# A decoder layer on one core: conditioning dots placed one per query block, and gate stores issued by ScalarE

## The chip, the cores and the metric

The kernel runs on one core of a Trainium2 chip. The core has five engines that run beside each other, each through its own list of instructions in order: TensorE (PE: matmuls, which write to PSUM, with the loads of its weights as PEld), VectorE (DVE), ScalarE (ACT), GpSimd (POOL) and SyncE (SP, which here only issues DMAs). Sixteen DMA engines move data between DRAM and the on-chip memory (SBUF). The metric is the device time of one execution in microseconds (us), as a median of several runs.

## The reference

One layer of a decoder: a token-mixing part (a convolution and a stick-breaking attention, merged by gates), then a SwiGLU part. Width and sequence length are 1024, with 8 heads of 64. What matters here is where the conditioning vector `c` goes in, and what the gates are:

```python
c_act = jax.nn.silu(c)
mod = c_act @ ada_w[l] + ada_b[l]
sh1, sc1, ga1, sh2, sc2, ga2 = [m[:, None, :] for m in jnp.split(mod, 6, axis=-1)]
h = rmsnorm(x, pre_mix_g[l]) * (1.0 + sc1) + sh1
y = hybrid_mixer(h, ...)
x = x + ga1 * rmsnorm(y, post_mix_g[l])
h = rmsnorm(x, pre_ffn_g[l]) * (1.0 + sc2) + sh2
y = swiglu_ffn(h, w_ffn_in[l], w_ffn_out[l])
x = x + ga2 * rmsnorm(y, post_ffn_g[l])
```

In `hybrid_mixer`, `merged = sigmoid(g_conv) * y_conv + sigmoid(g_att) * y_att`. Both sigmoids come from `h @ w_in`, as do the convolution's input and the queries, keys and values. In the attention, each key's weight is its own sigmoid times the product of (1 - sigmoid) over the keys between it and the query. So the scores of one block of queries pass through two sigmoids, a running product and a multiplication before they meet the values.

`sh1` and `sc1` are needed at once. `ga1`, `sh2` and `sc2` are not needed before the output projection of the mixer has been computed, and `ga2` only at the very end.

## The kernel before

The kernel keeps activations transposed: 8 tiles of 128 channels by 1024 tokens. Each operand of a matmul is split into a high and a low part (`hi`, `lo`), and a product is three matmuls. ACT mostly makes the high part (a copy with rounding), DVE or POOL the low one (a subtraction).

**Order of the work.** A scheduler builds each engine's list. It goes through the program with a modelled timeline, and gives an engine that is free the ready instruction that comes first in the program. `tc.high_priority(offset=...)` lets instructions count as if they came earlier; `SOONER` is 5000, and the attention (`head`) runs under it, so that it goes ahead of the products traced around it, which fill the gaps. On the chip each list then runs strictly in order, and so does SP's list of DMAs: a DMA that waits for its buffer or its data holds back all DMAs behind it.

**Stages.** (1) `sh1`, `sc1` and the normalised input, together with the first products (to line 291). (2) Attention with fillers (lines 318 to 564): for each of four pairs of heads `p`, the gated input of the convolution `glu(p)`, the transposed operands `t_ops`, the convolution `conv(p)`, and two heads by `attend`, with the next pair's queries and keys (`qk_pair`) in between. Behind the fourth pair come the last convolution, four plain gates (`PLAIN`), and the first two of seven products of six gate pairs (`GPAIRS`, lines 552 to 564). (3) The other five products of these gate pairs (`other_five`), with the layer norm of the convolution (`ln_all`) in between. (4) The convolution's projection `y_conv` for n = 0 to 7 (lines 697 to 722), then the attention's projection (lines 733 to 747). (5) The output projection and the SwiGLU part (from line 749 on).

**One head** (line 422) goes through four blocks `c` of 256 queries. For each half-block of 128 queries and up to 512 keys: PE computes scores `z`; ACT makes two sigmoids, `kap` and `beta` (lines 455 and 456); DVE turns `kap` into running products by a scan (line 459); POOL multiplies `beta` by them (line 461). Then PE transposes `beta` (line 471), ACT and DVE split the result into `ahi` and `alo` (lines 474 and 475), and PE multiplies both with the values (lines 480 and 481).

**The conditioning dots.** 32 columns of `mod` (16 to 47: `ga1`, `sh2`, `sc2`, `ga2`, eight each) are computed by `dot_c` (line 133): a weight tile of 128 x 1024 is loaded, and DVE multiplies it with the broadcast `cb` and sums along the row (line 135). Before, `ada2_dots(n)` (line 502) loads and computes `n` of them; it is called with 0, 4, 8 and 8 ahead of the four pairs of heads (line 536), with 2 behind each plain gate (line 546), and for what is left (line 547). The tiles have a tag of their own, `aw`, with two buffers. Nothing ties the dots to a place in DVE's list but their place in the program and those buffers. Lines 548 to 551 add the bias to all 32 columns and fold them with the norms' weights.

**The gate results.** Sigmoids of gates are written to DRAM (`s_d`, and a partial product in `e_d0`) and read back later. All these stores go through `load` (line 103), which issues on SP. Their source tiles (tag `sg`, two buffers, shared with the convolution's outputs) come free when the store has landed.

**Shared buffers.** The tag `wraw` has three buffers. Through them go the raw weights of all products by `load_w`, among them `wc` (convolution's projection) and `wa` (attention's projection), the gate pairs' weights (line 604) and the four `of` tiles with the attention's output (line 725).

Of the kernel before, what the change touches and what calls it, by code (L numbers as in the profile page):

```python
# [18 lines left out]
P = 128  # L19
# [31 lines left out]
SOONER = 5000  # L51
A2_AT = (0, 4, 8, 8)
EARLY = 9
# [22 lines left out]
def tile_block(ctx: ExitStack, tc: tile.TileContext, xT, vecs, crow, ada1, ada2, win, wv, wcv, wat, wo, w1, w2, cvw, out):  # L76
# [241 lines left out]
    with ExitStack() as sC:  # L318
        pc = mkpool(sC, "pc")
        with ExitStack() as sA:  # L320
# [101 lines left out]
            def head(p, hh, qst, kst, klo, vts, oT):  # L422
# [6 lines left out]
                for ci, c in enumerate(order):  # L429
# [5 lines left out]
                    for sc in range(nsc - 1, -1, -1):  # L435
                        probs = []
                        for i in (2 * c, 2 * c + 1):
# [20 lines left out]
                            init = 1.0 if diag else kap[:, s_hi:s_hi + 1]  # L458
                            dve.tensor_tensor_scan(rev, rev, rev, init, op0=ALU.mult, op1=ALU.bypass)  # L459
                            m = w - 1 if diag else w  # L460
# [21 lines left out]
                    if ci % 2 == 1:  # L482
                        cs = slice((c // 2) * CH, (c // 2 + 1) * CH)
                        act.activation(oT[half, cs], av[other], AF.Copy)
                        dve.tensor_tensor(oT[half, cs], av[half], oT[half, cs], op=ALU.add)  # L485

            def attend(p, qk, vts):
                qs, ks, kl = qk
                oT = pa.tile([P, T], F32, tag="oT", name=f"oT{p}", bufs=1)
                nxt = None  # L490
                for hh in range(2):
                    with tc.high_priority(offset=SOONER):
                        head(p, hh, qs[hh], ks[hh], kl[hh], vts, oT)
                    if hh == 0 and p < 3:
                        nxt = qk_pair(p + 1)
                with tc.high_priority(offset=SOONER):
                    load(o_d[p], oT)
                return nxt

            a2 = deque(range(2 * KT, 6 * KT))  # L500

            def ada2_dots(n):
                for _ in range(n):
                    col = a2.popleft()
                    w = pa.tile([P, D], F32, tag="aw", name=f"ada2_{col}", bufs=2)
                    load(w, ada2[col - 2 * KT])
                    dot_c(w, cb, col)
# [21 lines left out]
            for p in range(4):  # L529
                glu(p)  # L530
                if p == 2:
                    v = v_half(1)
                t_ops(p)
                if p < 3:
                    conv(p)
                ada2_dots(A2_AT[p])
                qk = attend(p, qk, v)
            conv(3)
            for n in PLAIN:
                gb = banks2(f"pg{n}")  # L540
                gemm(gb, load_w(win[20 + n], f"wg{n}"), h, range(KT))
                for c in range(NCH):
                    sg = sgp.tile([P, CH], F32, tag="sg", name=f"sg{n}_{c}", bufs=2)
                    act.activation(sg, gb[c], AF.Sigmoid, bias=0.0, scale=1.0)
                    load(s_d[n][:, c * CH:(c + 1) * CH], sg)
                ada2_dots(2)
            ada2_dots(len(a2))
            add_bias(16, 48)
            fold_gate(gpost1, 16, C_POST1)
            fold_scale(scale2, 32, C_PRE2)  # L550
            fold_gate(gpost2, 40, C_POST2)
            for i in GPAIRS:
# [5 lines left out]
                act.activation(e[0], k1, AF.Copy)  # L558
                load(e_d0[i], e[0])
                k2 = bank(f"k2_{i}")  # L560
                prod0(k2, w_op(f"a12_{i}", raw[:, CH:], act, pool), "B21")
                dve.tensor_tensor(e[1], k2, e[0], op=ALU.add)
                act.activation(e[1], e[1], AF.Sigmoid, bias=0.0, scale=1.0)
                load(s_d[2 * i][:, :CH], e[1])

    sV.close()
    with ExitStack() as sG:
# [45 lines left out]
        def sig_out(t, n, c):  # L613
            act.activation(t, t, AF.Sigmoid, bias=0.0, scale=1.0)
            load(s_d[n][:, c * CH:(c + 1) * CH], t)

# [104 lines left out]
        for n in range(KT):  # L721
            y_conv(n)
        ohi, olo = [], []
        for p in range(4):
# [573 lines left out]
```

## Time and profile before

| | |
|---|---|
| three runs | 1488.84, 1490.8, 1490.9 us; median 1490.8 us |
| the profiled execution | 1492.5 us |
| its span in the profile | 1490.7 us, 19082 instructions |
| DMA | 271.06 MB, mean 182 GB/s |

The prediction quotes rows of several views. A row of a *timeline* has the start, the busy time, engine, line, operation, output <- inputs, and in brackets the idle time of the engine before it with what ended it. A row by *stretch* has start:end and length, then the busy time of PE, PEld, DVE, ACT and POOL with the number of instructions, the clock granted to TensorE as a share of full speed, the share of time in which the 16 DMA engines were busy, and GB/s. A *wait* row says who waited for whom, for how long in total, how often, and the longest. Durations of an instruction are given as min/median/max in ns. "SPq" is SP's queue of DMA issues; "landing" is the time from a DMA's issue until its data have arrived.

### The profile page before, as it was taken

What the parts mean: (1) busy time and instruction counts of PE and PEld (TensorE: products, weight loads), DVE (VectorE), ACT (ScalarE), POOL (GpSimd) and SP (SyncE); (2) the same over time, 40 slices, a digit from 0 to 9 for tenths busy, and PEclk for the clock granted to TensorE, in tenths of its full rate; (3) what the DMA queues carried; (4) which work ended last, traced back from release to release, by engine and by line L of the source; (5) the groups of instructions that cost most, each with busy time, mean ns of one, the idle gap of its engine ahead of it and who ended that gap; (6) DMA issues with size and microseconds to landing.
All of it is one profiled execution on the core that took longest, in us unless ns stands there. A gap on an engine that the chain in (4) does not pass through costs nothing.

```text
span 1490.7 us, 19082 instructions
## 1 busy us (share of the span) xinstructions
PE 1402.0 (94%) x6888; PEld 1170.8 (79%) x6888; DVE 1016.2 (68%) x1440; ACT 654.3 (44%) x1138; POOL 310.5 (21%) x281
## 2 busy tenths in 40 slices
PE   5997999999999999899998949999999999999996
PEld 4886788898888777688886738887888887888886
DVE  7899877666481168837467697678778864764457
ACT  5363466446462335422445463334444443432541
POOL 0042535325162364333000000001111110000000
PEclk9999999999999999999999979999999999999999
DMA  9456444054045763643443623547777748666843
GB/s 383 167 186 189 151 155 144 26 184 134 23 142 195 278 210 122 232 157 109 152 145 132 224 92 128 170 156 264 258 249 259 255 134 287 235 227 193 286 128 113
DMA packets 98717, 271.06 MB, mean 182 GB/s; under 512 B 10048, under 2 KB 20416, under 8 KB 97600
## 3 DMA queue, kind: packets, MB, share of 16 engines
q1 hardware_dynamic: 88768, 235.24, 46.6%
q0 software_dynamic: 9856, 34.61, 6.0%
q8 instruction: 54, 0.88, 0.2%
q14 instruction: 39, 0.32, 0.1%
HBM read 196.41 MB, written 73.40 MB: 181 GB/s over the span
## 4 chain that ended last, share of the span: by engine, by line
PE 51%; DVE 4%; DMA 1%; ACT 0%; issue 0%; DVEq 0%; ACTq 0%
PE ka L892 14%; PE ka L1018 8%; PE kc L892 8%; PE pwo L180 5%; PE pb L1018 4%; PE pya L180 3%; PE pyc L180 3%; PE kb L892 2%; PE pa L1018 2%; PE ke L850 1%; DMA e_d<-e 1%; DVE y L831 1%; DVE e L855 0%; DMA w1u<-in_w_dram 0%; PE fsum L1225 0%
## 5 line engine op out<-in xcount | busy, mean ns | idle before, releaser
L461 POOL TENSOR_TENSOR be<-be,ka 128x127 f32<-128x127 f32 (+2 forms) x96 | 108.6, 1142 | 179.2 <-DVE ka L459 111.0
L459 DVE TENSOR_TENSOR_SCAN ka<-ka 128x128 f32<-128x128 f32 (+2 forms) x96 | 107.4, 1136 | 26.8 <-ACT ka L455 26.7
L107 POOL DMA_DIRECT2D g_d<-w x22 | 12.1, 552 | 413.1 <-DVE w L971 413.1
L455 ACT ACTIVATE ka<-z 128x128 f32<-128x128 f32 (+2 forms) x96 | 47.3, 495 | 66.5 <-PE z L454 30.8
L475 DVE TENSOR_TENSOR alo<-tr,ahi 128x512 fp32r<-128x512 f32 x80 | 52.8, 680 | 30.7 <-ACT ahi L474 30.5
L474 ACT ACTIVATE ahi<-tr 128x512 fp32r<-128x512 f32 x80 | 46.7, 602 | 39.7 <-PE tr L471 28.0
L892 PE MATMUL kc<-b,s4o 128*128 128x512 f32 x264 | 63.4, 389 | 0.0
L1018 PE MATMUL ka<-gt,w2f 128*128 128x512 f32 x264 | 63.4, 389 | 0.0
L1018 PEld LDWEIGHTS ka<-gt,w2f 128*128 128x128 f32 x264 | 49.6, 188 | 10.3
L892 PEld LDWEIGHTS kc<-b,s4o 128*128 128x128 f32 x264 | 49.6, 188 | 10.3
L471 PE MATMUL tr<-ident,be 128*128 128x128 f32 x288 | 50.6, 279 | 5.4 <-DVE alo L475 5.0
L850 PE MATMUL ke<-b,we_hi 128*128 128x512 f32 x144 | 50.0, 427 | 4.2 <-DVE b L161 2.5
L481 PE MATMUL av<-alo,vst 128*128 128x256 f32 x160 | 44.1, 299 | 9.3 <-DVE alo L475 9.2
L456 ACT ACTIVATE be<-z 128x128 f32<-128x128 f32 (+2 forms) x96 | 46.8, 498 | 10.1 <-PE tr L471 10.0
L135 DVE SCALAR_TENSOR_TENSOR ada<-ada,cb 128x1024 f32<-128x1024 f32 x32 | 45.2, 1414 | 8.2 <-DMA ada<-in_ada_dram 7.8
L180 PE MATMUL pwo<-mlo,wo_hi 128*128 128x512 f32 x128 | 50.2, 392 | 0.0
L180 PE MATMUL pwo<-mhi,wo_lo 128*128 128x512 f32 x128 | 50.2, 392 | 0.0
L180 PE MATMUL pwo<-mhi,wo_hi 128*128 128x512 f32 x128 | 49.8, 389 | 0.0
L480 PE MATMUL av<-ahi,vst 128*128 128x256 f32 x160 | 45.6, 299 | 1.7 <-DVE oT L485 1.2
L892 PE MATMUL ka<-b,a 128*128 128x512 f32 x156 | 40.7, 392 | 1.8 <-DVE a L883 1.8
L361 PE MATMUL pcv<-ph,cvw 128*128 128x128 f32 x320 | 41.6, 276 | 0.5 <-DMA ph<-v_d 0.5
L471 PEld LDWEIGHTS tr<-ident,be 128*128 128x128 f32 x288 | 35.5, 143 | 8.3 <-DVE alo L475 3.1
(484 smaller groups left out, 4127.6 us busy)
## 6 DMA issues: line engine op xcount, KB each, us to landing
w_d<-w2o POOLq DMA_DIRECT2D x44, 512.0 KB, 3.5
w2f<-w_d SPq DMA_DIRECT2D x44, 512.0 KB, 4.2
ada<-in_ada_dram SPq DMA_DIRECT2D x32, 512.0 KB, 3.7
w1g<-in_w_dram SPq DMA_DIRECT2D x22, 512.0 KB, 3.8
w1u<-in_w_dram SPq DMA_DIRECT2D x22, 512.0 KB, 4.3
w2r<-in_w_dram SPq DMA_DIRECT2D x44, 256.0 KB, 5.6
cvw<-in_cvw_dram SPq DMA_DIRECT2D x20, 512.0 KB, 3.8
ada_w<-in_ada_dram SPq DMA_DIRECT2D x8, 1024.0 KB, 12.3
```

What stands on the lines that cost most here:

```text
L180: pe.matmul(bank, st[:, cols], mv[k][:, c * CH:(c + 1) * CH], start=(i == 0 and s == 0), stop=(i == n - 1 and s == 2))
L455: act.activation(kap[:, s_lo:s_hi], z[:, zo:zo + w], AF.Sigmoid, bias=0.0, scale=-0.125)
L456: act.activation(beta[:, :w], z[:, zo:zo + w], AF.Sigmoid, bias=0.0, scale=0.125)
L459: dve.tensor_tensor_scan(rev, rev, rev, init, op0=ALU.mult, op1=ALU.bypass)
L461: pool.tensor_tensor(beta[:, :m], beta[:, :m], kap[:, s_lo + 1:s_lo + 1 + m], op=ALU.mult)
L471: pe.transpose(tr[:, o:o + P], src, ident)
L474: act.activation(ahi, tr, AF.Copy)
L475: dve.tensor_tensor(alo, tr, ahi, op=ALU.subtract)
L480: pe.matmul(avc, lhs, ahi[:, cols], start=(jp == c and jj == 0), stop=False)
L850: pe.matmul(kb, wf[st][:, cols], t[:, mv], start=(j == 0 and q == 0), stop=(j == HK - 1 and q == 2))
L892: pe.matmul(bank_, st[:, cols], t[:, mv], start=(first and j == 0 and s == 0), stop=(j == HK - 1 and s == 2), skip_group_check=not first)
L1018: pe.matmul(dst, w[st][:, cols], g[mv], start=first and s == 0, stop=last and s == 2, skip_group_check=more)
```

## The change

Three things are edited.

1. `head` becomes a generator. After each of its four blocks it hands back the block's last scan. In `attend`, from head 3 on (`2 * p + hh >= A2_HEAD` with `A2_HEAD = 2`, counted from 0), one dot follows each block: its load is traced with normal priority, and the dot itself stands in `tc.issue_after(scan.ins)`, which orders it behind that scan in DVE's list, without a wait between engines. That is 6 heads x 4 blocks = 24 dots, columns 16 to 39.
2. The last 8 dots (columns 40 to 47, `ga2`) follow the eight steps of `y_conv`, with their tiles in the tag `wraw`. The bias and the fold of these columns come after them; those of columns 16 to 39 stay where they were.
3. The 38 stores of gate results (8 of plain gates, 12 in the first two products of six gate pairs, 18 in `sig_out`) are issued by `act.dma_start`, on ACT's own DMA queue, instead of SP's.

```diff
-A2_AT = (0, 4, 8, 8)
+A2_HEAD = 2
...
-                            dve.tensor_tensor_scan(rev, rev, rev, init, op0=ALU.mult, op1=ALU.bypass)
+                            scan = dve.tensor_tensor_scan(rev, rev, rev, init, op0=ALU.mult, op1=ALU.bypass)
...
+                    yield scan
...
                 for hh in range(2):
+                    steps = head(p, hh, qs[hh], ks[hh], kl[hh], vts, oT)
+                    for _ in range(4):
+                        with tc.high_priority(offset=SOONER):
+                            scan = next(steps)
+                        if 2 * p + hh >= A2_HEAD:
+                            ada2_dot(scan)
                     with tc.high_priority(offset=SOONER):
-                        head(p, hh, qs[hh], ks[hh], kl[hh], vts, oT)
+                        assert next(steps, None) is None
...
-            a2 = deque(range(2 * KT, 6 * KT))
-
-            def ada2_dots(n):
-                for _ in range(n):
-                    col = a2.popleft()
-                    w = pa.tile([P, D], F32, tag="aw", name=f"ada2_{col}", bufs=2)
-                    load(w, ada2[col - 2 * KT])
+            a2 = deque(range(2 * KT, 5 * KT))
+
+            def ada2_dot(scan):
+                col = a2.popleft()
+                w = pa.tile([P, D], F32, tag="aw", name=f"ada2_{col}", bufs=2)
+                load(w, ada2[col - 2 * KT])
+                with tc.issue_after(scan.ins):
                     dot_c(w, cb, col)
...
-                ada2_dots(A2_AT[p])
...
-                    load(s_d[n][:, c * CH:(c + 1) * CH], sg)
-                ada2_dots(2)
-            ada2_dots(len(a2))
-            add_bias(16, 48)
+                    act.dma_start(s_d[n][:, c * CH:(c + 1) * CH], sg)
+            assert not a2
+            add_bias(16, 40)
             fold_gate(gpost1, 16, C_POST1)
             fold_scale(scale2, 32, C_PRE2)
-            fold_gate(gpost2, 40, C_POST2)
...
-                load(e_d0[i], e[0])
+                act.dma_start(e_d0[i], e[0])
...
-                load(s_d[2 * i][:, :CH], e[1])
+                act.dma_start(s_d[2 * i][:, :CH], e[1])
...
         def sig_out(t, n, c):
             act.activation(t, t, AF.Sigmoid, bias=0.0, scale=1.0)
-            load(s_d[n][:, c * CH:(c + 1) * CH], t)
+            act.dma_start(s_d[n][:, c * CH:(c + 1) * CH], t)
...
         for n in range(KT):
             y_conv(n)
+            w = wp.tile([P, D], F32, tag="wraw", name=f"ada2_{5 * KT + n}")
+            load(w, ada2[3 * KT + n])
+            dot_c(w, cb, 5 * KT + n)
+        add_bias(40, 48)
+        fold_gate(gpost2, 40, C_POST2)
```

## The prediction

> **What bounds the kernel now.** I read the page first, then the stretches, then the waits inside the stretches that the change touches.
>
> ```profile
> PE 1402.0 (94%) x6888; PEld 1170.8 (79%) x6888; DVE 1016.2 (68%) x1440; ACT 654.3 (44%) x1138; POOL 310.5 (21%) x281
> PE 51%; DVE 4%; DMA 1%; ACT 0%; issue 0%; DVEq 0%; ACTq 0%
> ```
>
> TensorE (PE) is busy for 1402.0 of 1490.7 us, and the chain that ended last runs mostly through it. None of its matmuls changes. The time can therefore only move where PE stands idle or runs at a reduced clock, and I look for these places. Here is the view of engine time by stretch (from and to, length, then busy time of PE, weight load, DVE, ACT and POOL, then the granted PE clock, DMA share, GB/s). The second fence is the same view for line 135 alone, the conditioning dots, and the third holds its durations:
>
> ```profile
> 60.00:176.00 116.00, 100.31 (x630) 87.35 (x630) 104.72 (x143) 53.17 (x108) 43.78 (x29) 0.96 0.60 191
> 176.00:456.00 280.00, 275.62 (x1696) 240.11 (x1695) 186.43 (x227) 157.44 (x322) 113.73 (x89) 1.00 0.34 113
> 540.00:628.00 88.00, 81.50 (x344) 64.19 (x344) 80.14 (x93) 46.15 (x68) 44.27 (x26) 0.99 0.46 157
> ```
>
> ```profile
> 60.00:176.00 116.00, 43.57 (x62) 0.96 0.60 191
> ```
>
> ```profile
> L135 DVE SCALAR_TENSOR_TENSOR ada<-ada,cb x32: 1191/1226/2108, 58.1 to 160.7; 128x1024 f32<-128x1024 f32 x32
> ```
>
> Stretch 60 to 176 holds the first V projection and heads 1 and 2. There VectorE (DVE) is busy for 104.72 of 116 us, and 43.57 us of that is dots (62 instructions, so 31 dots with their 31 accumulator reads: 1.41 us each). PE is idle for 116 - 100.31 = 15.7 us, and its clock averages 0.96, which costs another 0.04 x 116 = 4.6 us. In heads 3 to 8 (176 to 456) there is no dot, DVE is busy for 186.43 of 280 us (67%), and PE idles for 4.4 us at full clock. The waits of PE in the first stretch (who waited, for whom, total, times, longest) name the cause:
>
> ```profile
> PE av L481 <- DVE alo L475: 6.7, 6, 1.7
> PE tr L471 <- DVE alo L475: 4.8, 3, 2.7
> PE pv L381 <- DVE qst L405: 1.5, 2, 0.8
> PE z L451 <- ACT sg L290: 1.4, 1, 1.4
> ```
>
> 13.0 us of the 15.7 are waits for ordinary DVE work (`alo`, `qst`) that stands behind dots in a full, in-order queue. That is the first place. The second is at 491 us:
>
> ```profile
> 477.51 1.07 ACT L544 ACTIVATE sg<-pg 128x512 f32<-128x512 f32 x2
> ```
>
> ```profile
> 484.24 1.60 SPq L104 DMA_DIRECT2D s_d<-sg  x2
> ```
>
> ```profile
> DMA to landing us min/median/max: 8.9/9.2/9.5
> ```
>
> ```profile
> 488.11 0.39 PE L315 MATMUL k<-hhi,a 128*128 128x512 f32 x1
> ...
> 494.51 0.79 PE L315 MATMUL k<-hhi,a 128*128 128x512 f32 x1 [3.53 <-ACT sg L544]
> ```
>
> ```profile
> 495.00:500.00 5.00, 5.00 (x13) 3.84 (x13) 0.00 (x0) 0.08 (x1) 0.00 (x0) 0.50 0.99 395
> 500.00:505.00 5.00, 5.00 (x22) 4.05 (x22) 0.69 (x1) 2.39 (x4) 2.38 (x2) 0.93 0.39 75
> ```
>
> Two gate sigmoids end at 478.6. Their stores leave SP's queue only at 484.24, behind prefetches, and land 8.9 to 9.5 us later, at 493.7. Until then the two `sg` buffers are taken, so the next sigmoids cannot empty their PSUM banks, and PE waits 3.5 us. Then it runs at half clock: (1 - 0.50) x 5 + (1 - 0.93) x 5 = 2.9 us. Together 6.4 us.
>
> **The change part by part.**
>
> *A, 32 dots leave 60 to 176.* DVE there drops from 104.7 to about 61 us of 116 (53%). The loss was 15.7 + 4.6 = 20.3 us, or 0.65 us for each of the 31 dots. I keep 4.0: the 1.4 us wait for ScalarE (ACT), half of the `qst` wait (0.8), since those first evacuations come in a burst, and 1.8 for the rate of the later heads (4.4 / 280 x 116). Gain 16.3 us; bounds 8 (half) and 18.9 (all but the ACT wait). The 32 loads (32 x 512 KB) leave the stretch too, but at a DMA share of 0.60 nothing there waits for bandwidth. The bias and fold instructions that follow the last dot move out of this stretch as well.
>
> *B, 24 dots enter heads 3 to 8,* each behind the last scan of its query block. That adds 24 x 1.41 = 33.8 us: DVE goes from 186.4 to 220.2 of 280 us, 79%. Queued behind a dot stand the block's `alo` subtractions and the next block's scans, and PE, ACT and POOL wait for those. The next view shows what a loaded DVE costs PE, in stretches of 25 us:
>
> ```profile
> 75.00:100.00 25.00, 22.87 (x180) 21.59 (x180) 24.74 (x38) 16.27 (x35) 10.63 (x8) 1.00 0.60 187
> 100.00:125.00 25.00, 22.13 (x140) 19.06 (x138) 23.01 (x32) 9.55 (x21) 7.93 (x7) 1.00 0.54 171
> 200.00:225.00 25.00, 24.88 (x143) 20.84 (x142) 21.18 (x27) 16.06 (x34) 10.68 (x9) 1.00 0.50 182
> 225.00:250.00 25.00, 23.05 (x179) 20.90 (x178) 18.66 (x24) 17.02 (x40) 12.89 (x13) 1.00 0.45 138
> 275.00:300.00 25.00, 25.00 (x126) 20.30 (x125) 19.13 (x22) 12.43 (x26) 11.78 (x9) 1.00 0.00 1
> 400.00:425.00 25.00, 23.08 (x158) 20.06 (x157) 19.48 (x25) 15.66 (x35) 12.88 (x12) 1.00 0.19 64
> 425.00:450.00 25.00, 24.61 (x172) 22.11 (x171) 19.27 (x19) 16.48 (x38) 17.21 (x12) 1.00 0.56 169
> ```
>
> With DVE at 75 to 85% (the last five rows) PE idles 0.1, 2.0, 0, 1.9 and 0.4 us, 4.4 in all. About two dots, 3 us, come into each, which puts them at 87 to 97%, like the first two rows, where PE idles 2.1 and 2.9. At 2.5 each that is 12.5, so 8.1 us more than now. The six other stretches stay below 85% and add about nothing. A dot may float to a gap and is not bound to a crowded moment, so I take +7; bounds 0 and 24 x 0.65 = 15.6. The 24 loads are spread over 280 us, where the DMA share is 0.34. SP's queue holds each until the dot two before it has freed its buffer, and weight loads stand behind; blocks are 280 / 24 = 12 us apart, so I cost this at nothing. Without that cover it is part of the upper bound.
>
> *C, 38 stores move to ACT's queue* (8 plain gates, 12 in the six `B11`/`B21` pairs, 18 in `sig_out`). Issued right after their sigmoids, the stores of 478.6 land by 488.1 even if they still take 9.5 us, and the last plain gate's matmuls run into 488.1. The stall goes: -6 of 6.4. In exchange each issue holds ACT:
>
> ```profile
> L104 SPq DMA_DIRECT2D s_d<-gc x6: 319/327/424, 544.9 to 625.1; - x6
> ```
>
> ```profile
> SPq L104 <- ACT gc L614: 24.3, 5, 6.6
> ...
> SPq L104 <- ACT sg L544: 19.1, 5, 10.5
> ```
>
> No ACT issue exists in this trace; the row of SP gives 0.32 us, and I estimate 0.4 with the wait for ACT's own result: 38 x 0.4 = 15 us over some 175 us in which ACT is about half busy (46.15 of 88 in 540 to 628). What queues behind each issue are the next operand copies, for which PE's products wait. On the other side SP's loads no longer stand behind results of ACT (24.3 and 19.1 us of SP waiting in the two largest rows). I set these two against each other at 0, with -2 and +5 as bounds.
>
> *D, 8 dots and 8 loads of 512 KB enter the convolution's projection.*
>
> ```profile
> 618.00:668.00 50.00, 46.39 (x198) 38.01 (x197) 21.24 (x26) 12.51 (x14) 18.13 (x8) 0.97 0.67 240
> ```
>
> ```profile
> 603.53 4.52 SPq L104 DMA_DIRECT2D wc_raw<-in_wcv_dram  x2
> ```
>
> ```profile
> 616.11 2.40 POOL L169 TENSOR_TENSOR wc_lo<-wc_raw,wc_hi 128x1024 fp32r<-128x1024 f32 x1 [6.14 <-ACT wc_hi L159]
> ```
>
> ```profile
> 626.94 1.21 PE L180 MATMUL pyc<-clo,wc_hi 128*128 128x512 f32 x2 [3.61 <-DVE clo L654]
> ```
>
> ```profile
> 667.81 43.52 PE pya L180 x192
> ```
>
> ```profile
> ada<-in_ada_dram SPq DMA_DIRECT2D x32, 512.0 KB, 3.7
> ...
> yc<-s_d SPq DMA_DIRECT2D x8, 512.0 KB, 7.0
> ```
>
> From 628 on DVE has room (21.24 of 50 us busy). Two costs remain. First, PE enters this projection 3.6 us late behind DVE's `clo`, and before 628 DVE is full (80.14 of 88). Two of the three `wraw` buffers come free near 603 to 608, where two `wc` loads start now; two of the new loads can take them, and if their dots are ordered ahead of `clo` they cost up to 2 x 1.41 = 2.8. I take 1.5. Second, the eight tiles share those three buffers with the weights of both projections and the four `of` tiles, about 14 tiles before the first matmul of the attention projection (667.81). At 3.7 (landing of an `ada` load) + 1.4 each that is 14 / 3 x 5.1 = 24 us from 618.5, where the first weight's split ends and frees its buffer, and hidden; at 7.0 (a `yc` load) + 2.4 (POOL's part of a split) it is 44 us, to 662, which with the last split ends on the edge. I take 1.5, so +3 for D; bounds 0 and 18.
>
> Sum: -16.3 + 7 - 6 + 0 + 3 = -12.3 us. The profiled execution took 1492.5 us (span 1490.7), so it would become 1480.2. The median of the three runs is 1490.8, 1.7 below the profiled one, so 1490.8 - 12.3 = 1478.5. 0.2% of it, 3 us, is about what a measurement of this kernel can tell from no change.
>
> **The rivals.**
>
> *Heads 3 to 8 pay back the full price.* POOL's multiply after each scan has these rows in 60 to 176 and in 175 to 456:
>
> ```profile
> L461 POOL TENSOR_TENSOR be<-be,ka 128x512 f32<-128x512 f32 x8 | 15.3, 1927 | 14.3 <-DVE ka L459 11.2 <-ACT ahi L474 1.9 <-ACT be L456 1.2
> ```
>
> ```profile
> L461 POOL TENSOR_TENSOR be<-be,ka 128x512 f32<-128x512 f32 x24 | 31.0, 1304 | 44.0 <-DVE fo L524 18.6 <-DVE ka L459 11.2 <-ACT be L456 10.6
> ```
>
> Beside dots it takes 1.93 us, without them 1.30. The change puts each dot exactly where the multiply of the last scan starts: 24 x 0.62 = 15 us on the attention's chain, and the same 15.6 comes from 0.65 per dot. The result is -12.3 + 8.6 = -3.7, so 1487. For it: the two rows. Against it: in 176 to 456 PE has matmuls of other products between, and most delays of the chain cost it nothing. The Trainium skill, page "SBUF — State Buffer", section "Who interferes with whom", says that a DVE instruction with two SBUF inputs and a GpSimd instruction that reads SBUF exclude each other for the whole instruction, the later one waiting. By that rule a dot that starts first delays the multiply by its whole length; the two rows agree in sign with half of it.
>
> *The early idle time goes only by half,* since what moves up into the freed DVE (the transposed operands' subtractions) or ACT's own evacuations then end last: -12.3 + 8.1 = -4.2, so 1486.6. Against it: DVE falls to 53%, and ACT is busy for only 53.17 of 116.
>
> *Slower: the ring of three `wraw` buffers in the projections.* If the two early tiles keep their buffers until DVE has finished `clo` at 628, and loads land in 9.2 us as in the crowded time at 484, each of 14 tiles holds a buffer for about 9.2 + 2.4 = 11.6 us: 14 / 3 x 11.6 = 54 us from 628, so 682, plus 2.4 for the split of the first attention weight: 684.4 instead of 667.81, 16.6 us of idle PE. In place of the 1.5 counted for the ring that gives -12.3 + 15.1 = +2.8, and with one spell at half clock after it (2.9, as at 495) +5.7, so 1496.5. It decides the sign once the attention projection begins over 13.8 us later against the entry into the first projection. Against it: the DMA share in 618 to 668 is 0.67 on the mean, so loads should land faster than at 484.
>
> **How the numbers follow.** The forecast has 0.55, the full price in heads 3 to 8 0.2, the half gain 0.13, the ring 0.12. The second and third lie at 1487 with a spread of some 4 us, so a third of them falls within 3 us of no change; of the ring's cases a sixth does. Faster: 0.55 + 0.14 + 0.09 = 0.78; same: 0.06 + 0.04 + 0.02 = 0.12; slower: 0.10. Low end: A at 18.9, B at 0, C at 6.4, D at 0 would be 25.3 less, 1465.5; I stop at 1467. High end: the second and third rival with their spread, 1491, which leaves out most of the ring. The forecast's own part is 1468 to 1487.
>
> **What would show it.** Line 135 has nothing between 60 and 176 except what the queueing allows after head 2, 24 executions in heads 3 to 8, and 8 near the convolution's projection. In the first stretch PE's waits for `alo` fall from 11.5 to a few us, the clock reads 1.00, and heads 3 to 8 begin some 16 us earlier. PE idles 8 to 14 us in heads 3 to 8, with `alo` as releaser. The wait for `sg` of 3.5 us is gone, with no row of 0.50 behind it. PE enters the convolution's projection after at most 6 us of waiting. The forecast is wrong if PE still waits for `alo` in heads 1 and 2, if heads 3 to 8 idle above 15 us, or if the attention projection opens with a wait for `of` or `wa`.

## The result, and the profile after

The changed kernel takes 1496.98 us (median of 4 runs, 1495.33 to 1498.88), the kernel before 1489.82 on the same chip: ratio 1.0049, 95% interval 1.0037 to 1.0062. It is 7.2 us slower; the forecast was 12.3 us faster. The profiled execution took 1495.33 us, span 1493.6.

By stretch (columns as before), the changed kernel:

```profile
60.00:176.00 116.00, 108.16 (x690) 95.32 (x689) 70.92 (x88) 59.76 (x118) 36.42 (x30) 0.99 0.19 60
176.00:456.00 280.00, 269.34 (x1645) 232.35 (x1644) 219.17 (x266) 150.11 (x310) 127.84 (x88) 0.99 0.47 155
...
495.00:500.00 5.00, 0.51 (x1) 0.50 (x2) 0.00 (x0) 1.66 (x4) 3.71 (x3) 0.53 1.03 410
500.00:505.00 5.00, 5.00 (x13) 3.85 (x12) 0.69 (x1) 0.63 (x1) 0.00 (x0) 0.50 1.01 404
505.00:510.00 5.00, 5.00 (x22) 4.08 (x22) 0.69 (x1) 1.86 (x3) 1.29 (x1) 0.95 0.51 178
```

Read it as the prediction did, as *loss*: idle PE time plus (1 - clock) x length. In 60 to 176 it falls from 20.3 to 7.8 + 1.2 = 9.0 us, although DVE is now busy for only 71 of 116 us. In 176 to 456 it rises from 4.4 to 10.7 + 2.8 = 13.5. Of the 11.3 gained, 9.1 are gone again. (The clock is given to two digits, so a loss is good to 0.6 us in the first stretch and to 1.4 us in the second.) The stall near 490, which should have disappeared, has grown. PE's waits:

```profile
PE tr L471 <- DVE alo L475: 7.1, 5, 3.0
PE av L481 <- DVE alo L475: 4.6, 2, 3.0
PE pk L180 <- ACT wk_hi L159: 1.6, 1, 1.6
...
PE k L315 <- ACT ee L562: 7.3, 1, 7.3
PE lnm L675 <- POOL la L673: 4.0, 1, 4.0
PE k L315 <- DVE s4o L302: 3.8, 1, 3.8
```

The 3.5 us of waiting for `sg` have become 7.3 us for `ee`, a spell at half clock again behind it. ACT's own row of instructions tells why (timeline; ACTq is its queue of DMA issues):

```profile
484.17 1.07 ACT L550 ACTIVATE sg<-pg 128x512 f32<-128x512 f32 x2
485.13 0.63 ACT L159 ACTIVATE a<-ew 128x512 fp32r<-128x512 f32 x1
492.67 1.60 ACTq L551 DMA_DIRECT2D s_d<-sg  x2
494.40 1.67 ACT L159 ACTIVATE a<-ew 128x512 fp32r<-128x512 f32 x3 [8.64 <-DMA T4o<-t_d]
498.84 0.60 ACT L562 ACTIVATE ee<-k 128x512 f32<-128x512 f32 x1 [2.77 <-DMA s_d<-sg]
```

The sigmoids of the last plain gate run at 484.17, but their stores are issued only at 492.67. In between ACT does nothing for 8.64 us: 6.9 us until the first store is issued, the rest with the two issues. The profile puts the wait down to a load that has nothing to do with the stores: `T4o`, issued by SP. The trace's records of semaphores (counters on which a wait can stand) show the tie. In each kernel of this study, all DMAs that SP and ACT issue (540 here) count their landing on the same eight semaphores, and none is issued before the last one on its semaphore has landed. The store of 492.67 shares its semaphore with the `T4o` load issued at 480.87, which landed at 492.59; the second store, of 493.95, with one that landed at 493.87. Behind the waiting stores stand the operand copies (`a<-ew`) and the evacuation `ee`, for which PE waits. The `T4o` loads take

```profile
DMA to landing us min/median/max: 10.2/10.7/11.7
```

A second view is the path. From the timelines I take the starts of the first `z` product, of the first product on `T2o` (521.99 before, 522.01 after) and of the first `pya` (667.65 and 672.23), and the end of the span:

| kernel | z to T2o | T2o to pya | pya to end | loss 60-176 | loss 176-456 |
|---|---|---|---|---|---|
| before | 440.7 | 145.7 | 823.0 | 20.3 | 4.4 |
| changed | 441.2 | 150.2 | 821.3 | 9.0 | 13.5 |
| dots only | 445.4 | 146.4 | 820.1 | 13.0 | 13.3 |
| stores only | 440.3 | 149.1 | 824.9 | 19.5 | 4.4 |
| projection's 8 dots only | 433.0 | 145.8 | 819.5 | 14.3 | 4.3 |
| dots only, whole heads | 432.5 | 147.6 | 820.3 | 3.4 | 11.2 |

In the two profiled executions the difference is 2.9 us of span; the one before was 2.7 us above its median and the one after 1.6 below, which makes up the rest of the 7.2. So the first path, which should have shrunk by 15.3 us (A, B and C), is unchanged, and the second has grown by 4.5. (The split between the two depends a little on where the lists put the first `T2o` product; their sum does not.)

Each row is one execution, and the times of the kernel before in the second group of experiments alone lie between 1486.7 and 1494.0 us. In heads 1 and 2 the changed kernel and dots only have the same lists (551 of 553 matmuls from 81 to 176 stand in the same order) and nearly the same idle time, 7.8 and 8.4 us; their losses, 9.0 and 13.0, differ by the clock. A few us in one row carry little weight.

### The profile page after: what moved, and what is told of

Read it like the earlier page. It is cut to its first block, busy times and chain, and to the rows that moved or that the text cites. A ratio compares the mean times of both kernels' runs of the same rounds, so it can differ in the third digit from the quotient of the medians.

```text
span 1493.6 us, 19061 instructions
## 1 busy us (share of the span) xinstructions
PE 1399.3 (94%) x6888; PEld 1167.1 (78%) x6888; DVE 1025.0 (69%) x1441; ACT 656.0 (44%) x1138; POOL 316.1 (21%) x281
## 4 chain that ended last, share of the span: by engine, by line
PE 48%; DVE 5%; DMA 3%; issue 1%; ACT 1%; DVEq 0%; SPq 0%; ACTq 0%
PE ka L901 12%; PE ka L1027 8%; PE kc L901 7%; PE pwo L180 5%; PE pb L1027 4%; PE pya L180 3%; PE pyc L180 3%; PE ke L859 2%; PE pa L1027 2%; PE kb L901 2%; DMA w2r<-in_w_dram 1%; DMA w1u<-in_w_dram 1%; DMA e_d<-e 1%; ACT y L841 0%; PE k L315 0%
## 5 line engine op out<-in xcount | busy, mean ns | idle before, releaser
L461 POOL TENSOR_TENSOR be<-be,ka 128x127 f32<-128x127 f32 (+2 forms) x96 | 115.9, 1217 | 169.8 <-DVE ka L459 83.1
L459 DVE TENSOR_TENSOR_SCAN ka<-ka 128x128 f32<-128x128 f32 (+2 forms) x96 | 115.4, 1220 | 33.0 <-ACT ka L455 32.8
L901 PEld LDWEIGHTS kc<-b,s4o 128*128 128x128 f32 x264 | 49.6, 188 | 10.3
L1027 PEld LDWEIGHTS ka<-gt,w2f 128*128 128x128 f32 x264 | 49.6, 188 | 10.3
L135 DVE SCALAR_TENSOR_TENSOR ada<-ada,cb 128x1024 f32<-128x1024 f32 x32 | 50.6, 1582 | 8.5 <-DMA ada<-in_ada_dram 8.5
L456 ACT ACTIVATE be<-z 128x128 f32<-128x128 f32 (+2 forms) x96 | 46.3, 495 | 10.8 <-PE tr L471 10.7
```

The lines of the kernel that those rows point to most:

```text
L135: dve.scalar_tensor_tensor(w, w, 1.0, cb, op0=ALU.mult, op1=ALU.mult, accum_out=mod[:, col:col + 1])
L456: act.activation(beta[:, :w], z[:, zo:zo + w], AF.Sigmoid, bias=0.0, scale=0.125)
L459: scan = dve.tensor_tensor_scan(rev, rev, rev, init, op0=ALU.mult, op1=ALU.bypass)
L461: pool.tensor_tensor(beta[:, :m], beta[:, :m], kap[:, s_lo + 1:s_lo + 1 + m], op=ALU.mult)
L901: pe.matmul(bank_, st[:, cols], t[:, mv], start=(first and j == 0 and s == 0), stop=(j == HK - 1 and s == 2), skip_group_check=not first)
L1027: pe.matmul(dst, w[st][:, cols], g[mv], start=first and s == 0, stop=last and s == 2, skip_group_check=more)
```

## The experiments

Each time stands beside the kernel before on the same chip: 1489.8 in the first group, 1489.3, 1488.9, 1489.7 and 1489.7 in the others.

**First group: which part costs?** Dots without stores, stores without dots, and two other ways to issue.

Dots only (all 38 stores back on SP):

```diff
-    act.dma_start(s_d[n][:, c * CH:(c + 1) * CH], sg)
+    load(s_d[n][:, c * CH:(c + 1) * CH], sg)
```

> The 24 + 8 dots as in the changed kernel, all 38 stores back on SP. Theory (the stores cost: on ACT's in-order list the plain gates' stores wait for SP's T4o loads, 8.64 us, and operand copies stand behind them): the stall near 491 goes back to before's size (PE waits about 3.5 us for sg, one spell at half clock), the stretch from the first k product to the first product of T2o goes from 38.2 to about 34 us, and the time lies 3 to 9 us below the changed kernel, at 1488 to 1494, about level with the kernel before. Rival (the dots cost: heads 3 to 8 and the convolution's projection take back more than the early stretch gives): the time stays within 2 us of the changed kernel, 1495 to 1499.

Measured: 1496.16, ratio 1.0041 (1.0026 to 1.0057). The rival's number: the dots alone cost nearly as much as the whole change. The stall is there too, by another way. SP's list, then ACT's, then PE's wait:

```profile
490.07 4.16 SPq L104 DMA_DIRECT2D T1o<-t_d  x4
495.24 1.60 SPq L104 DMA_DIRECT2D s_d<-sg  x2
```

```profile
487.25 1.07 ACT L550 ACTIVATE sg<-pg 128x512 f32<-128x512 f32 x2
...
504.85 0.60 ACT L562 ACTIVATE ee<-k 128x512 f32<-128x512 f32 x1 [8.89 <-DMA s_d<-sg]
```

```profile
PE k L315 <- ACT ee L562: 10.3, 1, 10.3
```

The stores of 488.3 stand behind the T loads until 495.24 and land near 504.8. Here too the first store shares its semaphore with a `T4o` load, which landed at 495.17. So the eight semaphores hold the stores whether ACT or SP issues them.

Stores only (the kernel before with the 38 stores on ACT's queue):

> The kernel before with only the 38 stores moved to ACT's queue; dots as before. Theory (stores cost): an ACT copy or the issue itself waits 7 to 9 us near 490 for a transfer on SP's queue, the first k product to first T2o product takes 36 to 39 us instead of 33.9, and the time is 1493 to 1499, 3 to 9 slower than before. Rival (dots cost, stores harmless): between 1485 and 1491, the sg wait of 3.5 us gone as the prediction had it.

Measured: 1498.78, ratio 1.0059 (1.0039 to 1.0078): 9.0 slower. The theory's number, but only part of its mechanism: ACT stands 3.4 us for SP's load where 7 to 9 were expected, and z to T2o is no longer than before (440.3). The layer norm starts later (PE's wait for it was 1.5 us before):

```profile
493.83 0.63 ACT L159 ACTIVATE a<-ew 128x512 fp32r<-128x512 f32 x1 [3.43 <-DMA T4o<-t_d]
```

```profile
PE lnm L671 <- POOL la L669: 3.7, 1, 3.7
```

So dots and stores each cost 6 to 9 us alone, and 7.2 together. With the dots there, moving the stores takes 4.2 us from z to T2o (445.4 to 441.2) and puts 3.8 on T2o to `pya`. What the stores cost shows on that second path: 149.1 to 150.6 in all four kernels of this study with stores on ACT, at most 147.6 in the eleven with stores on SP or POOL, loads in the old order and no more than eight dots there. That is 3.4 of the 9.0 us in stores only, and 1.9 more stand behind `pya`; the rest shows in the medians alone.

The plain gates' stores on POOL, the others on SP:

```diff
-    load(s_d[n][:, c * CH:(c + 1) * CH], sg)
+    store(s_d[n][:, c * CH:(c + 1) * CH], sg)
```

> Dots as in the changed kernel; the 8 plain gates' stores are issued from POOL's queue, the other 30 from SP. POOL has neither operand copies for k nor loads at that time. Theory (what costs is whose list the store stands in): stores leave right after their sigmoids near 479 and 484, no PE wait for sg above 1 us and no k wait of 7 us, first k to first T2o product falls from 38.2 to 28 to 31 us, time 1483 to 1490, 4 to 8 below dots only. Rival (the stores' transfers themselves are slow beside the T loads, whoever issues them): a stall of 3 us or more stays between 485 and 505, and the time is that of dots only.

Measured: 1497.19, ratio 1.0045 (1.0028 to 1.0063). A miss: the two stores leave at 489.25, right behind their sigmoids (POOL's DMAs count on eight semaphores of their own), but the next store in SP's list, issued at 500.37, lands late instead:

```profile
509.96 0.60 ACT L562 ACTIVATE ee<-k 128x512 f32<-128x512 f32 x1 [11.30 <-DMA e_d<-ee]
```

The changed kernel with the T loads issued by POOL:

```diff
-    load(t.bitcast(F32), t_d[j][:, q])
+    store(t.bitcast(F32), t_d[j][:, q])
```

> The changed kernel, stores on ACT, but the 16 loads of T2, T3, T4 and T1 are issued from POOL's queue instead of SP's. Theory (ACT's store waited for these loads and for nothing else): ACT's wait of 8.64 us for T4o goes, its stores issue within 1 us of their sigmoids, first k to first T2o product falls from 38.2 to 29 to 34 us, and the time lies 3 to 9 us below the changed kernel, 1488 to 1494, unless POOL's issues, held for ag or lo work, delay the T loads. Rival (ACT's issue cost or the transfers): ACT's gap near 484 to 494 stays at 5 us or more and the time within 2 us of the changed kernel.

Measured: 1491.34, ratio 1.0020 (1.0004 to 1.0035), 5.6 below the changed kernel. As the theory had it: ACT's wait is gone, the stores follow their sigmoids. (SP's list loses 16 loads as well, so not all of the 5.6 us need be ACT's wait.)

```profile
486.90 1.07 ACT L550 ACTIVATE sg<-pg 128x512 f32<-128x512 f32 x2
487.51 0.33 ACTq L551 DMA_DIRECT2D s_d<-sg  x1
```

**Second group: the dots apart, and the burst of T loads.**

The kernel before, with only the last 8 dots in the convolution's projection:

> The kernel before with only the last 8 dots moved to the convolution's projection; 24 dots stay early, stores on SP. Theory (two of the eight stand in the normalization's chain on DVE): the entry into this projection or the s4o and lnm waits ahead of it grow by 2 to 4 us, the early stretch gives back 8 x 0.35 to 0.65 = 3 to 5, so the time is within 3 us of before, 1487 to 1493, and the path from the first T2o product to the first pya product takes 147 to 150 us instead of 145.7. Rival (D is hidden): that path stays within 1 us of 145.7 and the time is 3 to 5 below before.

Measured: 1479.38, ratio 0.9935 (0.9921 to 0.9950): 9.9 faster, more than either side expected. The path from T2o to `pya` is 145.8 against 145.7, so these dots cost nothing where they went. The first path is 7.7 shorter, and the loss in 60 to 176 is 6.0 less.

24 dots in the heads, the last 8 early (traced ahead of the first pair):

> 24 dots one per query block of heads 3 to 8, the last 8 dots early as in the kernel before, all stores on SP, nothing in the convolution's projection. Theory (heads 3 to 8 pay back all that the early stretch gives, and the burst of T loads, which starts when the attention ends, then meets the E products): the matmuls done by 460 us are within 10 of before's 2343, the stall near 490 to 505 is 8 to 12 us, the time 1490 to 1496, that is 0 to 4 below dots only by the share of D. Rival (the loss of dots only is D's): stall near 490 as before, time 1482 to 1488.

Measured: 1488.16, ratio 0.9991 (0.9978 to 1.0004), between the two. Loss 5.4 in 60 to 176 and 13.8 in 176 to 456; the wait for `ee` is 10.7 us.

T4 loads held behind the last plain gate's stores, T1 loads behind the first `e_d` store, in the kernel before and in dots only:

```diff
+    with tc.issue_after(held[b].ins) if b in held else ExitStack():
         load(t.bitcast(F32), t_d[j][:, q])
```

> The kernel before with one thing changed: on SP's list the T4 loads stand behind the last plain gate's stores and the T1 loads behind the first E product's store; dots and stores as before. Theory (the stall near 490 comes of the order of the list: 16 loads of 512 KB that are not needed before 522 stand ahead of the stores that free sg): the s_d stores issue within 1 us of their sigmoids and land in under 8 us, PE's wait for sg of 3.5 and the spell at half clock go, first T2o product 4 to 7 us earlier, time 1483 to 1487. Rival (the transfers are the bound, the order is not): another stall of the same size stands a few us later, time within 3 us of before.

> Dots only (24 + 8 dots moved, stores on SP) with the same two holds: T4 loads behind the last plain gate's stores, T1 loads behind the first E product's store. Theory (the 10.3 us wait for ee in dots only is the burst's): this wait falls below 3 us, first T2o product comes at 515 to 519 instead of 526.5, time 1484 to 1490, 6 to 12 below dots only. Rival (the dots alone cost it): the time stays within 3 us of dots only, at 1493 to 1499.

Measured: 1488.32, ratio 0.9997 (0.9984 to 1.0010), and 1497.77, ratio 1.0060 (1.0044 to 1.0075). The stall did come from the order: z to T2o falls to 432.8 and 434.7. But T2o to `pya` grows to 151.9 and 155.7, so little or nothing is left. The first `T2o` product comes 8.0 us earlier in the first of the two, but the layer norm of the convolution does not follow. Its last sum on PE, before and then with the hold:

```profile
581.24 1.12 PE L681 MATMUL lnv<-la,ones 128*128 128x512 f32 x2 [1.64 <-POOL la L679]
```

```profile
582.19 1.13 PE L685 MATMUL lnv<-la,ones 128*128 128x512 f32 x2 [0.45 <-POOL la L683]
```

Its four loads of `cr`, further back in SP's list, start only 3.7 us earlier (522.83 instead of 526.49), and what PE saved it spends waiting for this chain and the gates beside it. The time is the rival's, the reason the order of the list again: with only 8 dots in the projection `T2o` comes 7.7 us earlier too, but there the `cr` loads start at 518.08 and the same sum at 572.56, so the whole chain moves along.

**Third group: where dots are cheap.**

Dots behind the last two blocks of heads 3 to 8 only (12), 12 early, 8 in the projection:

```diff
-    if 2 * p + hh >= A2_HEAD:
+    if 2 * p + hh >= A2_HEAD and blk >= 2:
```

> Stores on SP; 12 dots early, 12 dots behind the last two query blocks of heads 3 to 8 (none behind the first two, which are short and follow each other within some 10 us), 8 dots in the convolution's projection. Theory (the dots at the start of a head are the price, since three or four stand there within 20 us): the matmuls between 180 and 460 us are at most 15 below before's 1694, where dots only lost 48; time 1478 to 1484. Rival (any dot in a head costs the same, 2 matmuls each): about 24 lost, the wait for ee of over 8 us stays, time 1486 to 1493.

Measured: 1487.63, ratio 0.9985 (0.9972 to 0.9998). Half the dots, and the loss in 176 to 456 is the same 13.5 us. Counts of matmuls in a fixed window turned out to be a poor measure, since kernels reach other work in it; from here on I go by loss. Neither side explains this: half the dots do not cost half the loss, and the first blocks are not what costs.

16 dots in the projection; 8 there and 8 in the output projection; 8 there with the stores on ACT:

```diff
+    for col in (4 * KT + n, 5 * KT + n):
+        w = wp.tile([P, D], F32, tag="wraw", name=f"ada2_{col}")
```

> Stores on SP; 16 dots early, none in the heads, 16 in the convolution's projection (two behind each of its eight products). Theory (a dot that leaves the early stretch is worth 0.6 us or more and costs nothing behind 628): 4 to 6 us below the kernel with 8 dots there (1479.4), 1473 to 1476. Rival (the three wraw buffers and DVE behind the normalization are full at 16): the attention projection opens with a wait or the normalization's chain ends later, path from first T2o to first pya product above 149 us, time 1479 to 1488.

> Stores on SP; 16 dots early, none in the heads, 8 in the convolution's projection, 8 in the second half of the output projection (720 to 866), where DVE is busy for 94 of 146 us. Theory: each moved dot worth about 0.6 us, the new place free: 1473 to 1476, not above the kernel with 16 in the convolution's projection. Rival (DVE also makes half of each output weight's split there, and a dot ahead of it holds PE): PE idles over 3 us more between 720 and 866, time 1478 to 1484.

> The kernel with only the 8 dots in the convolution's projection (1479.4), and in addition the 38 stores on ACT's queue. Theory (ACT's in-order list and later loads for the normalization cost 4 to 9 us by themselves; with 24 dots in the heads this was hidden in a stall that was there already): 1484 to 1489, and the path from first T2o to first pya product 149 to 151 us instead of 145.8. Rival (stores cost only about the 0.8 us by which the changed kernel differs from dots only): 1479 to 1482.

Measured: 1491.83 (ratio 1.0019, 1.0008 to 1.0031), 1498.40 (1.0065, 1.0047 to 1.0083) and 1489.08 (1.0002, 0.9990 to 1.0014). Both places gain on the first path (429.1 and 428.7) and lose more behind it. At 16 the ring of `wraw`, the prediction's slower rival, does decide:

```profile
PE pya L180 <- ACT wa_hi L159: 9.8, 1, 9.8
```

With 8 in the output projection, the time from its first product to the last `ke` product is 169.2 us against 153.5 in the kernel before, and PE waits there for DVE:

```profile
PE psx L837 <- DVE xsum L833: 12.6, 1, 12.6
```

The first two are slower than both sides expected. The third adds the stores to the best kernel so far, and all of its 9.9 us are gone: without dots in the heads, the stores cost 9 to 10 us, as in stores only.

**Fourth group: what is it in the heads, and is it the ring?**

The kernel with 24 dots in the heads and 8 early, first with these 24 dots on one tile loaded once, then with the loads kept and a product of one column in place of each dot (so the 24 columns' values are left out in both):

```diff
+    w, o = fixed
...
+    dve.scalar_tensor_tensor(o, w, 1.0, cb, op0=ALU.mult, op1=ALU.mult, accum_out=mod[:, col:col + 1])
```

```diff
-    dot_c(w, cb, col)
+    dve.tensor_tensor(mod[:, col:col + 1], w[:, :1], cb[:, :1], op=ALU.mult)
```

> The kernel with 24 dots in heads 3 to 8 and 8 early (1488.2), but the 24 dots all read one tile that is loaded once: the DVE work stays, 23 loads of 512 KB on SP's list are left out (and so the columns' true values). Theory (DVE's time is the price in the heads): matmuls between 180 and 460 us stay 40 to 50 below before's 1694 and PE idles 10 to 12 us there, as with loads; time within 2 us of 1488. Rival (the price is SP's list and the loads): under 20 lost, PE idles under 7 us there, time 1480 to 1484.

> The same kernel with the 24 loads kept and each of the 24 dots replaced by a product of one column (a short DVE instruction at the same place; the dots' values are left out). Theory (DVE's time is the price): under 15 matmuls lost between 180 and 460, PE idles 4 to 6 us there, time 1476 to 1482. Rival (SP's list and the loads): 40 to 50 lost, time within 3 us of 1488.

Measured: 1486.35 (0.9981, 0.9967 to 0.9995) and 1490.51 (0.9996, 0.9980 to 1.0012). By stretch, first dots without loads, then loads without dots:

```profile
176.00:456.00 280.00, 268.97 (x1635) 233.03 (x1634) 223.37 (x267) 148.22 (x307) 130.24 (x88) 0.98 0.34 111
```

```profile
176.00:456.00 280.00, 264.10 (x1605) 227.89 (x1604) 190.56 (x241) 146.75 (x305) 110.63 (x88) 0.98 0.45 149
```

Losses of 16.6 and 21.5 us, against 13.8 with both dots and loads. Without a single dot DVE is back at 191 us, and PE loses more, not less. But the scheduler has rearranged the rest. Of the 1645 matmuls that the kernel with dots and loads starts in this stretch, 1610 stand in the same order in dots only, but 1290 in dots without loads and 1383 in loads without dots. So neither kernel isolates what it was made for: what the dots' DVE time or their loads cost by themselves stays open.

16 dots behind the attention in two tiles of their own, free, and held behind the last `clo`:

```diff
-    w = wp.tile([P, D], F32, tag="wraw", name=f"ada2_{col}")
+    w = pg.tile([P, D], F32, tag="aw2", name=f"ada2_{col}", bufs=2)
```

> 16 dots early, 16 behind the attention in two tiles of their own instead of the three wraw buffers, stores on SP; nothing holds these dots, so they come soon after the last scan, from about 470 on. Theory (DVE is idle there, 0 to 8 us busy of 20): the path up to the first T2o product as with 16 in the projection (429 us from the first z product), no wait for wa at the attention projection, time 1472 to 1477. Rival (their 512 KB loads stand in the crowded list behind the T loads and push the loads for the normalization back, as the holds on T4 and T1 did): path from first T2o to first pya product above 150 us, time 1478 to 1488.

> The same 16 dots in two tiles of their own, but held on DVE behind the last clo subtraction, so that they run beside the convolution's and the attention projection. Theory (the loss with 16 dots in the projection was the ring of three wraw buffers, 9.8 us of waiting for wa): no wait for wa above 1 us, path from first T2o to first pya product 145 to 147.5 us, time 1473 to 1477. Rival (DVE or the transfers behind 628 are the bound, not the ring): path above 150 us or PE idle over 4 us between 664 and 720, time 1480 to 1490.

Measured: 1484.82 (0.9969, 0.9955 to 0.9982) and 1484.53 (0.9964, 0.9951 to 0.9976). The wait for `wa` is gone in both, so it was the ring; held, T2o to `pya` takes 145.1. But PE then waits 2.9 us for `mhi` at the output projection, the time is 7.5 us above the theory's 1473 to 1477, and 8 dots there remain better than 16. Free, the dots run early and the path is 151.4, as the rival had it.

**Fifth group: the tracing of the heads.** Up to here, all kernels that lose much in 176 to 456 trace a head in five raised-priority blocks, and all others in one. But the first also all pin something behind the scans, and the others nothing. The first kernel here keeps the five blocks without dots in the heads; the second keeps the dots:

```diff
-    for _ in range(4):
-        with tc.high_priority(offset=SOONER):
-            scan = next(steps)
-        if 2 * p + hh >= A2_HEAD:
-            ada2_dot(scan)
+    with tc.high_priority(offset=SOONER):
+        scans = list(steps)
+    if 2 * p + hh >= A2_HEAD:
+        for scan in scans:
+            ada2_dot(scan)
```

> The kernel with only 8 dots in the convolution's projection (1479.4), with one thing added: each head is traced as in the changed kernel, in a raised-priority block for each query block, but no dot stands between them. Nothing is computed otherwise; of some 7,890 instructions, the order of about 540 in the lists of the five engines is another (av products and transposes above all). Theory (what the heads lose is this order, since neither the dots' DVE time nor their loads was it): idle and clock loss of PE between 180 and 460 is 10 to 18 us instead of 4.3, time 1485 to 1492. Rival (a pinned instruction behind the scan is needed for the loss): 4 to 6 us there, time 1478 to 1481.

> Dots only (24 behind the same scans of heads 3 to 8, 8 in the convolution's projection, stores on SP; 1496.2), but each head is traced in one raised-priority block, as in the kernel before, and its four dots after it, pinned to the same four scans. Theory (the order that the blocks of the trace give was the price in the heads): idle and clock loss between 180 and 460 falls from 13.3 to 4 to 9 us, wait for ee under 6, time 1474 to 1483, the best of all with the dots out of the early stretch. Rival (dots or pins are the price): 12 to 16 us there, time 1492 to 1498.

Measured: 1486.22 (0.9978, 0.9965 to 0.9991) and 1483.33 (0.9964, 0.9949 to 0.9978). The second computes the same as dots only (1496.16), with the same pins, and is 12.8 us faster. What differs is the place in the program: a head is one block, and its four dots and their loads are traced behind the whole head. By stretch, dots only, then dots only with whole heads:

```profile
60.00:176.00 116.00, 107.60 (x676) 94.60 (x675) 68.27 (x84) 59.12 (x117) 36.39 (x30) 0.96 0.19 60
176.00:456.00 280.00, 269.48 (x1646) 232.66 (x1645) 219.95 (x269) 150.46 (x312) 129.51 (x88) 0.99 0.47 154
```

```profile
60.00:176.00 116.00, 112.57 (x718) 98.97 (x717) 71.87 (x92) 63.58 (x129) 37.15 (x30) 1.00 0.21 64
176.00:456.00 280.00, 271.60 (x1662) 235.28 (x1661) 219.96 (x265) 149.79 (x307) 137.33 (x89) 0.99 0.47 153
```

The same dots and the same DVE time, and the loss goes from 13.0 to 3.4 in heads 1 and 2 (where there is no dot at all), of which 5.0 us are idle time and the rest clock. In heads 3 to 8 it goes only from 13.3 to 11.2, where the theory wanted 4 to 9, and PE still waits 8.2 us for `ee`, where it wanted under 6:

```profile
PE k L315 <- ACT ee L560: 8.2, 1, 8.2
```

The lists differ: 433 of 553 matmuls from 81 to 176 stand in the same order, and 1305 of 1644 from 176 to 456. The waits of heads 1 and 2 show what another order does, dots only first:

```profile
PE tr L471 <- DVE alo L475: 3.8, 3, 2.5
PE pk L180 <- ACT wk_hi L159: 1.9, 1, 1.9
PE pq L180 <- ACT wq_hi L159: 1.5, 1, 1.5
```

```profile
PE av L481 <- DVE alo L475: 0.7, 1, 0.7
...
PE pq L180 <- ACT wq_hi L159: 0.4, 1, 0.4
```

The blocks without dots met the expected time but not the place: loss 11.6 and 5.3, about as with whole heads (14.3 and 4.3), and z to T2o is 0.8 us longer. Of the 6.8 us by which that kernel is slower than its twin, the profiles show 4.2 behind `pya`, where the lists of the two differ little. So in heads 3 to 8 the loss goes with what is pinned there, with either tracing, and five blocks alone do not bring it. Nor do five blocks fix the loss in heads 1 and 2: with 24 dots in the heads and 8 early it is 5.4, in yet another order (433 of the 553 in common with dots only). What is shown is that the way the dots are traced is worth 12.8 us; which part of the changed order costs it is not.

The best version is the kernel before with only the 8 dots in the convolution's projection: 1479.4 us, 0.65% below the kernel before and 17.6 below the changed one.

## Why the prediction was wrong, point by point

- *A, 16.3 us.* The changed kernel gained 11.3, dots only 7.3 (the difference is clock, not idle time). With whole heads the same move gains 20.3 - 3.4 = 16.9. The mechanism and the size were right; the edit that took part of it back was not priced at all.
- *B, +7.* The changed kernel lost 9.1 there, with whole heads 11.2 - 4.4 = 6.8. The size was right, the reason behind it is not shown: without the dots' DVE time the loss was larger (21.5), but in another order of everything else.
- *The failing step.* The prediction costs the dots, the stores and the buffers, but not the tracing of `head` as a generator in five priority blocks. It stands in the diff, and the document's own description says that the scheduler goes by program order and priority. It was priced at nothing without a word. Tracing the heads whole and the dots behind them is worth 12.8 us with these dots. That and C make up the miss: A, B and D forecast 6.3 us less and the whole-head kernel measured 6.3 less; the tracing adds 12.8, the stores 0.8 instead of -6. That the 6.3 agree so well is partly luck, since A, B and D by their own measured sizes give 10.0.
- *C, -6, the second failing step.* It has the stores "issued right after their sigmoids". A store on ACT's list is not issued after its sigmoid, but after everything for which it waits, and here that was SP's `T4o` load on the same semaphore (issued 0.08 us after it landed). In the kernel before it was no different: the store of 484.24, put down to prefetches ahead of it in SP's list, shares its semaphore with a `T3o` load that landed at 484.17. Another engine's list does not lead out of that. The 0.4 us per issue was right (0.33), but no measure of that. On the first path the stores gained some 0.3 us in stores only; behind it they cost 3.4, where the bound was +5, and in all 9.0 by the medians. With the dots, the stall was there anyway (10.3 us in dots only), and the stores added only 0.8: 4.2 less up to T2o, 3.8 more from there to `pya`, 1.2 more behind.
- *D, +3.* Measured 0.1, with only these 8 dots moved. PE's waits there changed places: `s4o` rises from 0.2 to 3.8, `clo` falls from 3.6 to 0.3.
- *The rival on heads 3 to 8.* The Trainium skill, page "SBUF — State Buffer", section "Who interferes with whom", has DVE and GpSimd exclude each other on a shared port. POOL's 128x512 multiply agrees: 1304 ns before, 1675 in the changed kernel, 1688 with dots without loads, 1334 with loads without dots. But the kernel with 1334 loses most, and the one with whole heads has 1851 and loses least of those with dots there. So the rule is seen, but the time of the multiply does not set the loss here; these kernels differ in order too.
- *The ring.* Its 12% were for this kernel, where PE has no wait for `wa` at all. That its 1496.5 us lie so near the measured 1497.0 is luck. With 8 dots in the projection PE does not wait for `wa`, with 16 it waits 9.8 us.

Open: why this scheduler orders `av` products and transposes otherwise under blocks than under one (the lists show that it does), and which of these changes costs the time; what a dot and its load cost in heads 3 to 8 in an unchanged order; the changed kernel's stores with whole heads, which was not run; and why the time behind the last `ke` product, for which the lists are nearly the same, varies from 622.2 to 628.4 us over these kernels.

## What to carry to other kernels

When instructions are slipped into a traced block, compare the lists of all engines before pricing the instructions: a changed order of everything else can cost more than what was added. The same holds for an experiment that takes something out: it isolates a cost only if the rest keeps its order. Moving DMAs to another engine's queue moves their waits onto that engine's list, so ask what stands behind them there and what they may wait for. Move few things at a time: eight of the 32 dots, in the last place, were worth 9.9 us, the whole change -7.2.

## What the runs showed of the hardware

ACT stood still for 8.64 us because a store on its list waited for a load issued by SP that shares no tile with it. Both count on one of eight semaphores that the program shares among all DMAs of SP and ACT; with those loads on POOL's queue the wait was gone and the store was issued 0.6 us after the start of its sigmoid. The Trainium skill, page "DMA: Bandwidth & Descriptors", section "Issuing engines are not separate DMA queues", says that issuing from several engines saves only the sequencer's time; the time saved on SP is indeed small (0.32 us per issue there, 0.33 on ACT). Whether a store lands sooner the runs do not settle: beside the T loads, gate stores took 6.1 to 6.8 us from ACT in the changed kernel, 6.6 to 7.2 from POOL, 6.9 to 9.5 from SP in the kernel before. They do show that the move can cost far more than it saves. And a dot of 1226 ns (median) took up to 3350 ns beside other work.
